# Adding up the squares of the first RMS norm: TensorE matmuls in one bank in place of GpSimd additions

## The chip, the cores and the metric

The kernel runs on one core of one Trainium2 chip, as one launch. The metric is the device time of a run in microseconds (us), lower is better. A core has TensorE for matmuls (PE in the profile, with its weight loads listed apart as PEld), VectorE (DVE), ScalarE (ACT), GpSimd (POOL) and SyncE (SP), which here only issues transfers. Each engine works through its own queue in order; a wait at the head of a queue holds everything behind it.

## The reference

Two layers of a decoder trunk over 512 tokens of 1024 features, everything in float32:

```python
def hybrid_layer(h, p_i, ...):
    xn = rms_norm(h, g_mix)
    proj = xn @ w_in                    # c_q, keys, values, gates, mLSTM inputs
    c_q = rms_norm(c_q, g_cq)           # then queries and index queries from c_q
    att = dsa_attention(...)            # top-k keys for each query, softmax, values
    hm = sigmoid(m_o) * rms_norm(mlstm_chunkwise(...), g_mh)
    h = h + concat([att, hm]) @ w_out
    h = h + square(relu(rms_norm(h, g_mlp) @ w_ff1)) @ w_ff2
    return h + sigmoid(rms_norm(h, g_ple) @ w_ple_gate + b) * (p_i @ w_ple)

def rms_norm(x, g):
    return x * rsqrt(mean(x * x, axis=-1) + 1e-6) * g
```

The change touches the first `rms_norm` of the first layer alone: the sum over 1024 features of the squares of each token.

## The kernel before

The state `h` lies feature-major: 8 blocks of 128 features (partitions) by 512 tokens. Float32 products are made of three single-precision passes: every operand is split into a rounded part `hi` (ACT) and a rest `lo` (DVE), and `mm3` or `token_step` issue hi·hi, hi·lo and lo·hi into one PSUM bank.

The norm is not applied before the projections. `prep` multiplies block k by the gain and splits it; the factor r of each token (the reciprocal root) is multiplied in when a projection is copied out of PSUM. So the matmuls need no r, but the copies after them do. `prep` also squares each block on ACT (L589) and adds the squares on GpSimd, seven additions in a chain (L594). `token_r` (L599) then multiplies the one sum with a column of ones: four float32 matmuls of a 128 x 128 block by one column, each giving the sums of 128 tokens in one column of a bank. From this bank DVE works out r in about a dozen tiny steps (`rsqrt`, L550), and `spread` (L613) makes a row of it.

Work is grouped in stages: mix, mlp and ple of layer 0 are stages 0, 1 and 2, those of layer 1 are 3, 4 and 5. The mix stage first projects `cq` (2 feature blocks: 8 x 2 x 3 = 48 matmuls of 512 columns) and `keys` (4 token blocks: 8 x 4 x 3 = 96 matmuls of 336 columns); then come the index queries, the top-k choice on DVE, queries, values, the convolution, attention, the mLSTM and the output projection. The squares of `cq` have a norm of their own, with four more one-column matmuls.

The program's order is made by a planner (`Plan.schedule`, L250). It goes through the work in simulated time with a cost for each operation and gives each free engine the ready operation of highest rank; the rank is the path to the end plus a thousand times the number that `URGENT` (L51) gives the operation's label. Labels that matter here are `start` 325 (splits of the first blocks and weights), `norm` 180, `squares0` 90, `cq` 80, `keys` 55, `queries` 45, `index` 30 and `values` 30. The order found is then written out as fixed, so on the chip each engine waits in that order whatever is ready. A buffer lives from its first writer to its last reader: weights come through three `raw` buffers, freed when DVE has made the `lo` part, into four `hi` and four `lo` buffers, freed when the last matmul has read them. Of the 8 PSUM banks, the 4 of keys and the 2 of cq are in use early on. All instructions are written out at one line (L395), so the profile tells them apart by tiles: `s` are 128 x 512 buffers, `raw`, `hi`, `lo` weights, `const` what stays (h, gains, ones), `ps_tr` a bank for norms and transposes.

Of the kernel before, what the change touches and what calls it, by code (L numbers as in the profile page):

```python
# [27 lines left out]
NTB = S // 128  # L28
# [378 lines left out]
class Trunk:  # L407
# [159 lines left out]
    def prep(self, l, gcol, forms=None):  # L567


        nc = self.nc  # L570
        label = nc.label
        cf = self.cf[l][0]
        xs, acc, last = [], None, None
        for k in range(KD):
            nc.label, nc.bias = ("prep", 0) if nc.stage else ("start", -STEP * k)
            hi, lo = self.slot([128, S], F32R), self.slot([128, S], F32R)
            self.split_block(self.h[k], cf[:, gcol + k:gcol + k + 1], hi, lo)
            if forms is not None:
                nc.label = "forms"
                x = self.slot([128, S])  # L580
                nc.scalar.activation(x, self.h[k], AF.Copy, scale=cf[:, gcol + k:gcol + k + 1])
                if k % 2:
                    forms.append(self.right_sums(last, x))
                last = x
            nc.bias = 0
            xs.append((hi, lo))
            nc.label = "squares" if nc.stage else "squares0"
            sq = self.slot([128, S])
            nc.scalar.activation(sq, self.h[k], AF.Square)  # L589
            if acc is None:  # L590
                acc = sq
            else:
                nacc = self.slot([128, S])
                nc.gpsimd.tensor_tensor(nacc, acc, sq, op=ALU.add)  # L594
                acc = nacc
        nc.label = label
        return xs, acc

    def token_r(self, acc, dim):  # L599

        nc = self.nc
        label, nc.label = nc.label, "norm"
        ps = self.psum("tr")
        for tb in range(NTB):
            nc.tensor.matmul(ps[:, tb:tb + 1], acc[:, tb * 128:(tb + 1) * 128], self.ones[:, 0:1],
                             start=True, stop=True)
        v = self.tiny([128, NTB])
        nc.vector.tensor_scalar(v, ps[:, 0:NTB], 1.0 / dim, EPS, op0=ALU.mult, op1=ALU.add)
        r = self.rsqrt(v, [128, NTB])
        nc.label = label  # L610
        return r
# [818 lines left out]
```

## Time and profile before

| | |
|---|---|
| median of 3 runs | 1330.98 us (1330.89 to 1331.20) |
| the profiled execution: its own time | 1332.49 us |
| the profiled execution: span from first to last instruction | 1330.5 us |
| mean granted TensorE clock | 0.996 |
| TensorE busy | 1305.7 us (98%) |
| VectorE busy | 1016.6 us (76%) |
| ScalarE busy | 725.2 us (55%) |
| GpSimd busy | 141.5 us (11%) |

The profiled execution took 1.5 us longer than the median of the runs; 2.0 us of it lie outside the span. The busy time of PE counts a matmul from its start to its modelled end, so two that overlap look busy without a gap; the distance from one weight load to the next is the better price of a matmul. The granted clock is 1.00 where TensorE has its higher level (2.4 GHz) and 0.50 at its lower (1.2 GHz).

### The profile page before, as it was taken

Reading aid. Unit: us, or ns where it says so; the run is one execution under the profiler, and the core shown is the slowest. Engines: PE = TensorE matmul, PEld = TensorE weight load, DVE = VectorE, ACT = ScalarE, POOL = GpSimd, SP = SyncE. Lnnn points to the kernel's source line nnn. Section 1 sums busy time; section 2 is a strip of 40 time slices with the busy share of each in tenths; the row PEclk is TensorE's granted clock in tenths of the full one; section 3 lists DMA queues with packets and bytes.
Section 4 is the critical chain, followed back from the end, with each engine's and each line's share of the span. In section 5 each row is a group of like instructions: output and inputs, shape, how many; then the busy total and the mean of one; then the engine's idle time right before and its main releaser. Section 6 shows DMA issues by size and latency. Waiting matters only on the chain. (4 is left out here: it accounts for less than half of the span.)

```text
span 1330.5 us, 19866 instructions
## 1 busy us (share of the span) xinstructions
PE 1305.7 (98%) x7376; PEld 1124.3 (85%) x7376; DVE 1016.6 (76%) x2122; ACT 725.2 (55%) x1403; POOL 141.5 (11%) x161
## 2 busy tenths in 40 slices
PE   6999999999999999999999999999999999999998
PEld 5877889888989899988887777988898898899887
DVE  7799997697777767763858999968877777767635
ACT  4887586474444434355448955847644444434542
POOL 4132000120000000004113211003000000000210
PEclk9999999999999999999999999999999999999999
DMA  5547610353323332335234674113433323333441
GB/s 195 119 112 181 159 49 2 95 127 111 97 95 111 96 111 82 109 127 130 82 100 114 140 176 112 48 33 99 124 107 99 111 90 101 96 111 95 127 121 70
DMA packets 41569, 141.76 MB, mean 107 GB/s; under 512 B 4992, under 2 KB 5504, under 8 KB 41472
## 3 DMA queue, kind: packets, MB, share of 16 engines
q1 hardware_dynamic: 34848, 116.37, 27.7%
q0 software_dynamic: 6624, 24.12, 9.9%
q8 instruction: 58, 0.95, 0.3%
q14 instruction: 39, 0.32, 0.1%
HBM read 114.25 MB, written 2.10 MB: 87 GB/s over the span
## 5 line engine op out<-in xcount | busy, mean ns | idle before, releaser
L395 PE MATMUL ps_proj<-s,hi 128*128 128x512 f32 (+1 forms) x3184 | 845.0, 355 | 2.7 <-DVE s L395 2.3
L395 PEld LDWEIGHTS ps_proj<-s,hi 128*128 128x128 f32 x3184 | 557.5, 189 | 90.7 <-DVE s L395 2.7
L395 PE MATMUL ps_proj<-s,lo 128*128 128x512 f32 (+1 forms) x1592 | 560.5, 355 | 0.5 <-DVE lo L395 0.5
L395 ACT ACTIVATE hi<-raw 128x1024 fp32r<-128x1024 f32 (+1 forms) x212 | 222.4, 1052 | 309.3 <-PE ps_proj L395 264.8
L395 PEld LDWEIGHTS ps_proj<-s,lo 128*128 128x128 f32 x1592 | 300.0, 189 | 45.6 <-DVE lo L395 1.3
L395 DVE TENSOR_TENSOR lo<-raw,hi 128x1024 fp32r<-128x1024 f32 (+1 forms) x165 | 202.9, 1230 | 83.9 <-ACT hi L395 76.3
L395 DVE TENSOR_TENSOR const<-const,ps_proj 128x512 f32<-128x512 f32 x160 | 109.6, 686 | 90.7 <-PE ps_proj L395 90.5
L395 PE MATMUL ps_proj<-hi,s 128*128 128x512 f32 (+1 forms) x384 | 112.8, 380 | 8.3 <-ACT hi L395 7.5
L395 POOL TENSOR_TENSOR s<-s,s 128x512 f32<-128x512 f32 x42 | 63.1, 1502 | 506.7 <-ACT s L395 494.5
L395 PEld LDWEIGHTS ps_proj<-hi,s 128*128 128x128 f32 x384 | 69.9, 193 | 18.7 <-ACT hi L395 7.5
L395 ACT ACTIVATE s<-s 128x512 fp32r<-128x512 f32 (+2 forms) x138 | 78.2, 620 | 13.8 <-DVE s L395 9.2
L395 PE MATMUL ps_sc<-s,s 128*128 128x512 f32 (+3 forms) x288 | 84.3, 375 | 0.6 <-ACT s_idx L395 0.2
L395 DVE TENSOR_TENSOR s<-s,s 128x512 fp32r<-128x512 f32 (+2 forms) x108 | 68.1, 667 | 9.0 <-ACT s L395 9.0
L395 POOL DMA_DIRECT2D lo<-raw x46 | 40.2, 873 | 295.8 <-ACT lo L395 237.3
L395 PE MATMUL ps_proj<-lo,s 128*128 128x512 f32 (+1 forms) x192 | 65.9, 382 | 1.8 <-DVE lo L395 1.7
L395 ACT ACTIVATE s<-const,const 128x512 fp32r<-128x512 f32 x64 | 44.2, 713 | 35.0 <-DVE const L395 35.0
L395 DVE SCALAR_TENSOR_TENSOR s<-const,const,s 128x512 fp32r<-128x512 f32 x48 | 48.0, 1009 | 17.0 <-ACT s L395 17.0
L395 ACT ACTIVATE s<-ps_proj 128x256 f32<-128x256 f32 (+1 forms) x104 | 42.8, 420 | 32.9 <-PE ps_proj L395 32.5
L395 PEld LDWEIGHTS ps_sc<-s,s 128*128 128x128 f32 x288 | 50.5, 190 | 8.8 <-ACT s_idx L395 1.5
L395 ACT ACTIVATE hi<-at 128x1024 fp32r<-128x1024 f32 x28 | 29.7, 1061 | 51.4 <-PE ps_proj L395 47.5
L395 DVE TENSOR_TENSOR s<-s,ps_proj 128x256 f32<-128x256 f32 x84 | 35.2, 419 | 26.7 <-PE ps_proj L395 23.3
L395 ACT ACTIVATE lo<-raw 128x1024 fp32r<-128x1024 f32 x46 | 48.8, 1062 | 9.7 <-PE ps_proj L395 6.0
(150 smaller groups left out, 1603.6 us busy)
## 6 DMA issues: line engine op xcount, KB each, us to landing
raw<-ws SPq DMA_DIRECT2D x204, 512.0 KB, 3.5
lo<-raw POOLq DMA_DIRECT2D x46, 512.0 KB, 5.1
raw<-wa SPq DMA_DIRECT2D x8, 336.0 KB, 3.6
const<-xt SPq DMA_DIRECT2D x8, 256.0 KB, 4.6
s<-pt SPq DMA_DIRECT2D x8, 256.0 KB, 4.6
out<-const SPq DMA_DIRECT2D x7, 256.0 KB, 2.0
const<-ct SPq DMA_DIRECT2D x2, 132.0 KB, 3.2
out<-const SPq DMA_DIRECT2D x2, 128.0 KB, 1.7
```

Of the source, the lines that this page charges most:

```text
L395: ins = getattr(getattr(nc, e), method)(*[value(x) for x in args], **{k: value(x) for k, x in kw.items()}).ins
```

## The change

In stage 0 the squares are no longer added by GpSimd. `prep` hands the list of the eight squares on, and `token_r` issues four one-column matmuls for each of them, all 32 into the same four columns of one bank, which TensorE adds up in PSUM. The first matmul of the first block alone opens the bank (`start`), those of the last block close it. In all other stages the sum is made as before, and `cq`, `keys` and the rest are not touched.

```diff
@@ prep
             sq = self.slot([128, S])
             nc.scalar.activation(sq, self.h[k], AF.Square)
-            if acc is None:
+            if not nc.stage:
+
+                acc = (acc or []) + [sq]
+            elif acc is None:
                 acc = sq
             else:
                 nacc = self.slot([128, S])
@@ token_r
         ps = self.psum("tr")
-        for tb in range(NTB):
-            nc.tensor.matmul(ps[:, tb:tb + 1], acc[:, tb * 128:(tb + 1) * 128], self.ones[:, 0:1],
-                             start=True, stop=True)
+        parts = acc if isinstance(acc, list) else [acc]
+        for k, part in enumerate(parts):
+            for tb in range(NTB):
+                nc.tensor.matmul(ps[:, tb:tb + 1], part[:, tb * 128:(tb + 1) * 128], self.ones[:, 0:1],
+                                 start=k == 0 and (tb == 0 or len(parts) == 1), stop=k == len(parts) - 1,
+                                 skip_group_check=len(parts) > 1)
```

The planner takes every operation anew, so the written order can change wherever its simulated times do.

## Rows read from the trace of the kernel before

**Rows 1.** The page's part 1: busy time, share of the span, instructions of each engine.
```profile
PE 1305.7 (98%) x7376; PEld 1124.3 (85%) x7376; DVE 1016.6 (76%) x2122; ACT 725.2 (55%) x1403; POOL 141.5 (11%) x161
```

**Rows 2.** Stretches of the first mix stage: busy us of each engine, granted clock, DMA.
```profile
core 0: us, PE busy (x) PEld busy (x) DVE busy (x) ACT busy (x) POOL busy (x), PEclk, DMA share, GB/s
25.00:29.00 4.00, 4.00 (x11) 3.14 (x12) 4.00 (x36) 0.00 (x0) 0.00 (x0) 0.57 0.75 243
30.40:37.10 6.70, 6.70 (x32) 5.57 (x31) 0.00 (x0) 1.62 (x3) 0.00 (x0) 1.00 0.00 0
54.00:60.00 6.00, 4.67 (x28) 3.81 (x29) 4.96 (x27) 6.00 (x23) 0.00 (x0) 1.00 0.67 158
60.00:80.00 20.00, 19.86 (x118) 16.43 (x117) 18.12 (x55) 18.16 (x65) 7.56 (x5) 1.00 0.36 80
80.00:100.00 20.00, 17.24 (x90) 13.42 (x89) 19.81 (x54) 17.01 (x44) 5.41 (x7) 1.00 0.50 122
100.00:104.00 4.00, 4.00 (x12) 3.11 (x11) 4.00 (x15) 3.77 (x9) 1.03 (x3) 0.57 1.04 240
```

**Rows 3.** Who waited for whom from 0 to 40 us: total us, times, longest.
```profile
PEld ps_proj L395 <- DVE lo L395: 3.7, 4, 1.6
```

**Rows 4.** Groups by shape: DVE and POOL to 20.1 us, then DVE from 20.1 to 24.95.
```profile
L395 DVE SCALAR_TENSOR_TENSOR s<-const,const,s 128x512 fp32r<-128x512 f32 x7 | 10.1, 1479 | 1.3 <-ACT s L395 1.3
L395 DVE TENSOR_TENSOR lo<-raw,hi 128x672 fp32r<-128x672 f32 x4 | 5.1, 1276 | 0.4 <-ACT hi L395 0.4
...
L395 POOL TENSOR_TENSOR s<-s,s 128x512 f32<-128x512 f32 x7 | 11.0, 1578 | 4.1 <-ACT s L395 3.9
...
L395 DVE TENSOR_TENSOR lo<-raw,hi 128x672 fp32r<-128x672 f32 x1 | 0.8, 846 | 0.0
```

**Rows 5.** Timeline of ACT, DVE and SP's transfers: start us, us, operation.
```profile
4.42 0.61 ACT L395 ACTIVATE s<-const 128x512 f32<-128x512 f32 x1
...
6.16 0.61 ACT L395 ACTIVATE s<-const 128x512 f32<-128x512 f32 x1
...
14.44 0.71 ACT L395 ACTIVATE s<-const,const 128x512 fp32r<-128x512 f32 x1
...
15.05 1.14 ACT L395 ACTIVATE s<-const 128x512 f32<-128x512 f32 x2
...
18.37 2.79 SPq L395 DMA_DIRECT2D raw<-ws  x2
...
20.73 0.74 DVE L395 SCALAR_TENSOR_TENSOR s<-const,const,s 128x512 fp32r<-128x512 f32 x1
...
21.95 1.06 ACT L395 ACTIVATE hi<-raw 128x1024 fp32r<-128x1024 f32 x1 [4.19 <-DMA raw<-ws]
...
23.73 1.22 DVE L395 TENSOR_TENSOR lo<-raw,hi 128x1024 fp32r<-128x1024 f32 x1
...
36.07 1.06 ACT L395 ACTIVATE hi<-raw 128x1024 fp32r<-128x1024 f32 x1 [3.99 <-PE ps_proj L395]
```

**Rows 6.** Timeline of TensorE's weight loads, one for each pass: start us, us, count.
```profile
7.48 1.06 PEld L395 LDWEIGHTS ps_proj<-hi,s 128*128 128x128 f32 x4 [7.48 <-ACT hi L395]
...
15.54 1.27 PEld L395 LDWEIGHTS ps_proj<-hi,s 128*128 128x128 f32 x8
...
21.57 1.01 PEld L395 LDWEIGHTS ps_tr<-const,s 128*128 128x128 f32 x8
...
33.58 0.87 PEld L395 LDWEIGHTS ps_proj<-s,hi 128*128 128x128 f32 x4
...
42.69 0.19 PEld L395 LDWEIGHTS ps_up<-hi,s 128*128 128x128 f32 x1
```

**Rows 7.** The norm of layer 1: its one-column passes (PEld), then the stretch behind them.
```profile
678.13 0.97 PEld L395 LDWEIGHTS ps_tr<-const,s 128*128 128x128 f32 x8 [1.37 <-POOL s L395]
...
680.00:684.00 4.00, 4.00 (x12) 3.10 (x12) 2.78 (x13) 0.00 (x0) 0.00 (x0) 0.57 0.00 0
```

## The prediction
> **What bounds the kernel now.** I read the page's busy shares first, then the first mix stage in stretches, then who waited for whom, the groups by shape, and the timeline engine by engine. TensorE is busy for 1305.7 of 1330.5 us [rows 1], so a microsecond of matmuls put into a full stretch costs a microsecond, and the question is how much idle or slow TensorE time lies where the change works. There is some in the first 43 us. The 144 matmuls of keys and cq, which the first index matmul at 42.69 us stands behind, begin at 7.48 us [rows 6]: 35.2 us. Their content I price by the distance of weight loads, (length of a run - 0.19) / (count - 1), where 0.19 us is one load. A 336-column matmul takes (1.27 - 0.19) / 7 = 0.154 us, a 512-column one (0.87 - 0.19) / 3 = 0.227, and a one-column float32 matmul makes two passes of (1.01 - 0.19) / 7 = 0.117, so the four of one block take 0.94 us [rows 6], in layer 1 0.89 [rows 7]; I take 0.92. Keys are 96 x 0.154 = 14.8, cq 48 x 0.227 = 10.9, the norm of the squares 0.92, that of cq 0.92, the two 512-column matmuls of `spread` 0.45: 28.0 us. So 7.2 of the 35.2 us are lost. Waits for a rest (`lo`) from VectorE take 3.7 [rows 3]; from 25 to 29 us the granted clock is 0.57, which costs 4 x 0.43 = 1.7 [rows 2]; the other 1.8 is the slow beginning, whose first four key matmuls stand (1.06 - 0.19) / 3 = 0.29 apart instead of 0.154 [rows 6], and small waits.
>
> VectorE is late because of GpSimd. While the seven additions run (11.0 us, mean 1578 ns), the rest of a block takes 1479 ns on VectorE, and that of a keys weight 1276 [rows 4]; with GpSimd idle they take 737 (0.74) [rows 5] and 846 ns [rows 4]. VectorE's row of rests ends at 20.73 + 0.74 = 21.47 us, though ScalarE had the last block's `hi` done at 14.44 + 0.71 = 15.15 [rows 5]. The lateness goes on through the buffers: the transfer of cq's second weight is issued only at 18.37, when a rest has freed its `raw` buffer; ScalarE waits 4.19 us for it and has its `hi` at 23.0, VectorE its `lo` at 24.95 [rows 5]. From 30.4 to 37.1 us VectorE then has nothing at all to do [rows 2]: ScalarE's next copy is held until cq's last matmul frees a weight buffer at 36.07 [rows 5].
>
> **What is removed.** Seven GpSimd additions, 11.0 us of an engine that is busy for 11% of the span: worth nothing by themselves. Their shadow on VectorE is worth more. At the idle prices the last rests end at 15.15 + 0.85 + 0.74 = 16.7 us at the latest, instead of 21.47. ScalarE's row is unchanged, since the same 8 squares and 12 `hi` parts stay in it. The third keys rest, which frees the buffer for cq's second weight, then comes 4 to 5 us earlier, and with it that weight: its `lo` is ready at about 20 instead of 24.95. One more thing goes: all squares are done at 15.05 + 1.14 = 16.2 us [rows 5], and the norm no longer waits for a chain of additions behind them.
>
> **What is added.** 28 one-column matmuls, 56 passes: 7 blocks x 0.92 = 6.4 us of TensorE. Where do they lie? The label `norm` (180) ranks over cq (80) and keys (55), so each block of four goes into TensorE's order soon after its square. Block 0's square is ready at 4.42 + 0.61 = 5.03 us, block 1's at 6.77 [rows 5], when TensorE has not begun: its first key matmul waits for ScalarE until 7.48 [rows 6]. These two blocks are mostly hidden by that wait. What a one-column pass takes at the beginning's slow rate no row shows: between 0.92 us for a block, as at full speed, and twice that, 1.84, as with the 336-column matmuls (0.29 against 0.154). So block 1 ends between 6.77 + 0.92 = 7.7 and 5.03 + 2 x 1.84 = 8.7 us. The other six stand among key matmuls and are on the path. The rest of the work is then 6 x 0.92 = 5.5, keys 14.8, cq 10.9, cq's norm 0.92, `spread` 0.45: 32.6 us, ending between 40.3 and 41.3 if TensorE neither waits nor slows.
>
> The waits for VectorE I take at nothing, because with 6.4 us more to do TensorE is now behind VectorE (rests done by 16.7, cq's by 20, while keys alone would fill it to 23): if that cover failed they would cost up to the 3.7 of now. The slow beginning costs between 0 (TensorE starts 2.4 us sooner, and may be at speed sooner) and the 1.8 of now; I take 0.9. The dip at 25 to 29 us, behind TensorE's waits, I take as gone, since no wait is left ahead of it. That gives 41.2 to 42.2, middle 41.7; 0.3 more for the new waits of TensorE for a square at the head of its queue (behind such a wait stand key matmuls that could have run; a square takes 0.61 and ScalarE runs ahead of TensorE) makes 42.0 instead of 42.69 us: a gain of 0.7. The bank that the norm opens is now held from the first block to the last, beside keys' four and cq's two; an eighth is left for `spread`, so it costs nothing. The squares live longer in buffers; the additions' outputs, one for each, go.
>
> **What is moved.** cq outranks keys, and its weights come 5 us earlier, so its 10.9 us now run from about 20 to 31 and the keys end last. The buffer that ScalarE waited for until 36.07 then comes 5 us earlier, and VectorE and ScalarE can do the rests and copies behind cq in their idle 6.7 us [rows 2]. After 42.69 TensorE still has idle time: 1.3 us from 54 to 60, 0.1 to 80, 2.8 to 100, and a clock of 0.57 from 100 to 104 costs 1.7 [rows 2]: 5.9 us, while VectorE is at 18.1 and 19.8 of 20 us [rows 2]. How much of it closes no row shows. Between all of it (-5.9) and as much again lost by a new written order (+3, half the sum); I take a gain of 0.7, nearer to nothing because the copies of keys, which lead to the top-k chain, cannot come earlier than the keys matmuls. Beyond 104 us TensorE is nearly gapless and shifts as a whole.
>
> The sum: -0.7 - 0.7 = -1.4 us. On the profiled execution's 1332.49 us that is 1331.1; against the median of the runs, 1330.98, from which that execution stood off by 1.5 us, it is 1329.6.
>
> **The clock speaks against the change.** From 5 to 17 us about half of TensorE's time would be one-column passes. Behind the only norm block of layer 1, which follows a wait of 1.37 us, the granted clock is 0.57 for 4 us [rows 7], though TensorE then ran without a gap; behind a block and waits it is 0.57 at 25 to 29 as well [rows 2]. The Trainium skill, "TensorE: Matmul & The Clock Gate", section Part 1: The HAM clock gate, says that the default state is throttled and that activity releases it. It does not say that a one-column matmul counts like a wide one; by that rule, if it does not, the start stays slow. This is the first rival.
>
> **The rivals.**
> Slower: the clock stays at 1.2 GHz (half) through the interleaved stretch, until cq's wide matmuls come. The price: some 30 key matmuls x (0.29 - 0.154) = 4.1 us, and the six blocks 0 to 5.5 more; against the forecast's 0.9 for a slow beginning and without its later gain, -0.7 - 0.9 + 4.1 = +2.5 at least, taken as +3.5: 1334.5. It decides if the half rate lasts beyond about 15 us. Against it: the key matmuls came to speed within 8 us of their start although they waited for VectorE.
> Faster: the later idle closes. With VectorE and ScalarE ahead by 5 us at 37, 3.5 of the 5.9 us go: -0.7 - 3.5 = -4.2, 1326.8; with all of it and no slow beginning 1323.5.
> It does not do what it says: if the blocks are not spread but stand together behind the last square, the two first are not hidden; then TensorE starts at 7.48 with 34.4 us of work and 1.8 lost: 43.7, +1.0, and the median is 1332.0. What speaks for it is that cq's norm matmuls stand together now; against it, their inputs come together.
>
> **How the numbers follow.** A measurement of this kernel can tell about 0.2% (2.7 us) from no change: faster is below 1328.3, slower above 1333.6. The forecast (1328.4 to 1332 with its bounds) has 0.36, the faster rival 0.32, blocks together 0.08, the slow clock 0.16, and 0.08 goes to a written order that loses more than it gains (+3 on top of the forecast's start: 1333.9). That makes faster 0.32, same 0.44, slower 0.24. The forecast is 1329.6. The range leaves out the lower end of the faster rival and the upper end of the slow clock, about 1 in 10 each: 1325 to 1335.5.
>
> **What the profile afterwards would show.** Right, if VectorE's rests of blocks fall from 1479 to about 740 ns, its row ends before 17 us, cq's second `lo` is ready near 20, one-column loads count 64 in the first 20 us, beginning near 5.0, GpSimd has 154 instructions and TensorE 7432, and the first `ps_up` load comes near 42. Wrong, if the granted clock or the distance of key matmuls shows half speed after 12 us (then the first rival), if `ps_up` is near 42 but the idle after 54 us differs much from 4.2 us (then the moved order decides), or if TensorE waits for squares by more than 1 us.

## The result, and the profile after

The changed kernel takes 1339.56 us (median of 4 runs, 1339.02 to 1339.99) against 1330.93 for the kernel before (four runs as well): 8.6 us more, a ratio of 1.0062 with a 95% interval of 1.0050 to 1.0073. The forecast was 1329.6. The span of its profiled execution is 1337.5 us, 7.0 more than before.

The page's part 1 of the changed kernel, as [rows 1]:

```profile
PE 1316.1 (98%) x7432; PEld 1138.8 (85%) x7432; DVE 1010.6 (76%) x2125; ACT 725.7 (54%) x1400; POOL 131.2 (10%) x154
```

TensorE has the 56 passes more that the change says, and 10.4 us more busy time. GpSimd has lost its seven additions, and VectorE is relieved, as this group by shape (5 to 20.1 us, of after; to be read beside [rows 4]) shows:

```profile
L395 DVE SCALAR_TENSOR_TENSOR s<-const,const,s 128x512 fp32r<-128x512 f32 x8 | 5.9, 748 | 2.6 <-ACT s L395 2.6
L395 DVE TENSOR_TENSOR lo<-raw,hi 128x672 fp32r<-128x672 f32 x4 | 3.4, 859 | 1.5 <-ACT hi L395 1.5
```

The rest of a block takes 748 ns and not 1479, that of a keys weight 859 and not 1276. VectorE's last rest of a block, in its timeline:

```profile
15.48 0.75 DVE L395 SCALAR_TENSOR_TENSOR s<-const,const,s 128x512 fp32r<-128x512 f32 x1
```

ends at 16.2 us instead of 21.5. What went wrong stands on TensorE. This is the timeline of its weight loads in the changed kernel (start us, us, count), with the first index matmul at the end, as in [rows 6]:

```profile
5.74 3.49 PEld L395 LDWEIGHTS ps_tr<-const,s 128*128 128x128 f32 x16 [5.74 <-issue]
9.11 0.33 PEld L395 LDWEIGHTS ps_proj<-hi,s 128*128 128x128 f32 x1
9.36 1.85 PEld L395 LDWEIGHTS ps_tr<-const,s 128*128 128x128 f32 x8
...
12.71 1.89 PEld L395 LDWEIGHTS ps_tr<-const,s 128*128 128x128 f32 x8
...
22.03 3.60 PEld L395 LDWEIGHTS ps_tr<-const,s 128*128 128x128 f32 x16
25.51 0.33 PEld L395 LDWEIGHTS ps_proj<-lo,s 128*128 128x128 f32 x1
25.72 2.29 PEld L395 LDWEIGHTS ps_proj<-hi,s 128*128 128x128 f32 x8
27.97 1.17 PEld L395 LDWEIGHTS ps_proj<-lo,s 128*128 128x128 f32 x4
...
31.32 0.19 PEld L395 LDWEIGHTS ps_proj<-lo,s 128*128 128x128 f32 x1
...
51.33 0.19 PEld L395 LDWEIGHTS ps_up<-hi,s 128*128 128x128 f32 x1
```

Three things are to be seen. From 5.74 us on TensorE waits for nothing. One weight load takes 0.33 us until about 30 us and 0.19 later. And everything is slow alike until then: the passes of a block stand (1.89 - 0.33) / 7 = 0.223 us apart instead of 0.117, the key matmuls (2.29 - 0.33) / 7 = 0.28 instead of 0.154. That is the lower clock, 1.2 GHz, for some 24 us. The profile's granted clock does not say so here: it reads 1.00 throughout, as it also does over the slow first key matmuls of before; it seems to hold no reading before the first change that it records. The length of a load is the better witness, and `e3_in_a_row` below shows both together.

The sum closes on this to 0.4 us. 64 passes x (0.223 - 0.117) = 6.8 us, and the 38 key matmuls issued up to 29.9 us x (0.28 - 0.154) = 4.8: 11.6 us lost. The work at full speed was 34.4 us. 34.4 + 11.6 = 46.0, and from 5.74 to 51.33 us are 45.6. The first index matmul comes 8.6 us later than before.

Further on, some of this is made up. These are the `ps_pn` matmuls before and after (first and last start, us):

```profile
L395 PE MATMUL ps_pn<-vx,s_d x160: 272/275/349, 169.6 to 867.4; 128*128 128x129 f32 x160
L395 PE MATMUL ps_pn<-vx,s_d x160: 272/275/329, 177.5 to 874.4; 128*128 128x129 f32 x160
```

The first is 7.9 us later than before and the last 7.0, as the spans are. So it is in part by accident that 8.6 us is also the difference of the medians: the profiled execution of before was 1.5 us above its median. The idle time that the forecast hoped to close is not what made it up. The stretch from 54 to 104 us of before, and the same length 8 us later after the change (columns as in [rows 2]):

```profile
54.00:104.00 50.00, 45.77 (x242) 36.77 (x243) 46.89 (x148) 44.95 (x137) 13.99 (x14) 0.97 0.51 119
62.00:112.00 50.00, 45.81 (x243) 37.10 (x242) 48.55 (x148) 45.15 (x133) 13.29 (x13) 0.97 0.46 102
```

TensorE is idle for 4.2 us in both, and the mean granted clock is 0.97 in both: the idle time and the dip that stood at 100 us are still there, 8 us later (the granted clock is 0.60 from 108 to 112 us). Behind the norm of layer 1, where [rows 7] show 0.57 for 4 us, it is 1.00 in this execution (688 to 692 us), which may account for the last 0.9 us.

### The profile page after: what moved, and what is told of

It reads as the page before. It is cut to its first block, busy times and chain, and to the rows that moved or that the text cites. A ratio compares the mean times of both kernels' runs of the same rounds, so it can differ in the third digit from the quotient of the medians.

```text
span 1337.5 us, 19963 instructions
## 1 busy us (share of the span) xinstructions
PE 1316.1 (98%) x7432; PEld 1138.8 (85%) x7432; DVE 1010.6 (76%) x2125; ACT 725.7 (54%) x1400; POOL 131.2 (10%) x154
## 5 line engine op out<-in xcount | busy, mean ns | idle before, releaser
L395 PE MATMUL ps_proj<-hi,s 128*128 128x512 f32 (+1 forms) x384 | 116.2, 389 | 3.3 <-ACT s L395 3.3
L395 POOL TENSOR_TENSOR s<-s,s 128x512 f32<-128x512 f32 x35 | 52.5, 1500 | 502.8 <-ACT s L395 491.2
L395 DVE SCALAR_TENSOR_TENSOR s<-const,const,s 128x512 fp32r<-128x512 f32 x48 | 42.0, 881 | 18.1 <-ACT s L395 18.1
```

The source lines that it names most:

```text
L395: ins = getattr(getattr(nc, e), method)(*[value(x) for x in args], **{k: value(x) for k, x in kw.items()}).ins
```

## The experiments

My theory after reading this profile, the clock theory: one-column passes do not bring TensorE to its higher clock, and the blocks among the first key matmuls keep it at the lower one. Rivals: the work theory (a one-column float32 pass takes its 0.22 us by itself), the order theory (the planner's new order and GpSimd's missing part are the loss), and that taking the sum to TensorE is bad in itself.

**e1_neither** takes the additions away and adds nothing. In stage 0 the norm is made from the last block's squares:

```diff
-            nc.scalar.activation(sq, self.h[k], AF.Square)
-            if acc is None:
+            nc.scalar.activation(sq, self.h[k], AF.Square, scale=1.0 if nc.stage else 8 ** 0.5)
+            if acc is None or not nc.stage:
```

> Neither the GpSimd additions nor the added matmuls: the norm is taken from the last block's squares alone, scaled by 8, so seven blocks are left out of the sum. Clock theory (the change loses because one-column passes keep TensorE at its lower clock): without such passes key matmuls are 0.154 us apart by about 12 us, the first ps_up load comes at 38 to 39 us instead of 42.7 (before) and 51.3 (after), and the time is 1326 to 1328. Order theory (the change loses by the new written order and the loss of GpSimd's part as such): the first ps_up load near 43, the time 1331 or more. Work theory (the passes cost their 0.21 us each whatever the clock) gives the same as the clock theory here.

Measured: 1324.67 us against 1331.13, ratio 0.9948 (0.9933 to 0.9963). Two of its first weight loads, then those of the index matmuls (min/median/max ns, first and last start in us):

```profile
6.33 1.06 PEld L395 LDWEIGHTS ps_proj<-hi,s 128*128 128x128 f32 x4 [6.33 <-ACT hi L395]
...
12.00 1.26 PEld L395 LDWEIGHTS ps_proj<-hi,s 128*128 128x128 f32 x8
```

```profile
L395 PEld LDWEIGHTS ps_up<-hi,s x28: 187/188/190, 36.5 to 47.4; 128*128 128x128 f32 x28
```

The first index matmul stands at 36.5 us, 6.2 earlier than before: better than I expected. So what the change removes is worth 6.5 us, and doing without GpSimd's additions, with the new order that this brings, loses nothing. That speaks against the order theory; the changed kernel's own order is put to the test in e6_columns.

**e2_both** keeps GpSimd's additions beside the changed kernel's 32 matmuls.

```diff
                 acc = (acc or []) + [sq]
+                if last is not None:
+                    nacc = self.slot([128, S])
+                    nc.gpsimd.tensor_tensor(nacc, last, sq, op=ALU.add)
+                    sq = nacc
+                last = sq
```

> The 32 matmuls of the change, and GpSimd's seven additions kept beside them (their sum is not used). Clock theory: as after, passes about 0.21 us apart and half rate until about 28 us; VectorE's rests are slow again (1.3 to 1.5 us) but TensorE is slower still and does not wait for them; first ps_up load 51 to 53, time 1339 to 1341. If taking GpSimd's additions away were the cause, the time would be 1331 to 1334.

Measured: 1340.49 us, ratio 1.0066 (1.0049 to 1.0082). VectorE's groups by shape (5 to 21 us) show it slow again:

```profile
L395 DVE SCALAR_TENSOR_TENSOR s<-const,const,s 128x512 fp32r<-128x512 f32 x8 | 8.8, 1125 | 2.3 <-ACT s L395 2.3
L395 DVE TENSOR_TENSOR lo<-raw,hi 128x672 fp32r<-128x672 f32 x4 | 7.2, 1802 | 0.4 <-ACT hi L395 0.4
```

The index matmuls' loads:

```profile
L395 PEld LDWEIGHTS ps_up<-hi,s x28: 186/187/190, 50.8 to 65.0; 128*128 128x128 f32 x28
```

but the first index matmul stands at 50.8, no later than in the changed kernel. The matmuls alone make the loss; and VectorE's relief, worth 6.5 us in e1_neither, is worth at most 1 us behind a TensorE that is later still.

**e3_in_a_row** turns the order of the blocks, so that the first of the 32 matmuls needs the last square and none can stand among the early key matmuls.

```diff
-        parts = acc if isinstance(acc, list) else [acc]
+        parts = acc[::-1] if isinstance(acc, list) else [acc]
```

> The same 32 matmuls, but the block of the last square first, so that all stand in one row behind the last square (16 us) and none among the early key matmuls. Clock theory: the keys in front come to 0.154 us by about 12 us as in before, the 64 passes take 0.117 us each (7.5 us), the clock falls behind them for some 4 us (1.7 lost); first ps_up load 43.5 to 46, time 1331.5 to 1335. Work theory (the passes cost 0.21 us each wherever they stand): 64 passes take over 13 us, first ps_up load near 51, time 1338 to 1341. Order theory: near 1339 too if keys and cq are pushed back as much.

Measured: 1337.35 us, ratio 1.0040 (1.0025 to 1.0055): a miss for all three. The five runs are spread, two at 1334.2 and 1335.0, three from 1337.4 to 1338.6; the profile is of the run of 1337.35. The weight loads show what happened, and here the granted clock has been recorded (the second fence is of stretches, with the columns of [rows 2]):

```profile
14.40 1.26 PEld L395 LDWEIGHTS ps_proj<-hi,s 128*128 128x128 f32 x8
...
15.93 1.01 PEld L395 LDWEIGHTS ps_tr<-const,s 128*128 128x128 f32 x8
...
17.12 10.22 PEld L395 LDWEIGHTS ps_tr<-const,s 128*128 128x128 f32 x56
```

```profile
17.50:20.00 2.50, 2.50 (x21) 2.50 (x21) 2.28 (x18) 0.00 (x0) 0.00 (x0) 0.84 0.85 261
20.00:30.00 10.00, 10.00 (x42) 9.42 (x42) 3.92 (x35) 1.06 (x1) 1.15 (x2) 0.50 0.38 92
```

The keys in front come to 0.154 us as before, and the first block's passes take 0.117 us, on the same squares and the same bank: the work theory is out. But in the row the granted clock falls to 0.50 while TensorE is busy without a gap, and stays there through the wide matmuls of cq that follow, until about 33 us. I had the clock fall behind the row; it fell inside it, so the 56 passes took 10.2 us, and the fall cost more than 1.7.

**e4_wide** lets TensorE add the squares with wide matmuls: one of 512 columns with the identity for each block, a copy of the bank, and then the four one-column matmuls of before. The squares are rounded for the single pass (the line for this is left out here).

```diff
...
+        if isinstance(acc, list):
+            total = self.psum("tr")
+            for k, part in enumerate(acc):
+                nc.tensor.matmul(total, self.identr, part, start=k == 0, stop=k == len(acc) - 1)
+            acc = self.slot([128, S])
+            nc.scalar.activation(acc, total, AF.Copy)
         ps = self.psum("tr")
-        parts = acc if isinstance(acc, list) else [acc]
+        parts = [acc]
```

> The sum still on TensorE and not on GpSimd, but by one 512-column single-precision matmul with the identity for each block (8 in all, into one bank), a ScalarE copy of the bank, and the old four one-column matmuls. The squares are rounded to single-pass precision. Clock theory: TensorE begins at about 5.7 us with wide matmuls, is at speed by 10 us and stays there; eight matmuls cost 0.23 to 0.45 us each; first ps_up load 39 to 41, time 1327 to 1329.5. If taking the sum to TensorE is the loss in itself (work on the full engine, or the new order), the time is above 1333.

Measured: 1327.09 us, ratio 0.9971 (0.9961 to 0.9982): faster than both kernels. Its weight loads in order of time, then those of the index matmuls:

```profile
5.89 0.29 PEld L395 LDWEIGHTS ps_tr<-s,const 128*128 128x128 f32 x1 [5.89 <-ACT s L395]
...
9.92 1.28 PEld L395 LDWEIGHTS ps_proj<-hi,s 128*128 128x128 f32 x8
11.21 0.19 PEld L395 LDWEIGHTS ps_tr<-s,const 128*128 128x128 f32 x1
```

```profile
L395 PEld LDWEIGHTS ps_up<-hi,s x28: 186/188/190, 37.4 to 50.8; 128*128 128x128 f32 x28
```

TensorE begins at 5.89, loads take 0.19 from 10 us on, and the first index matmul stands at 37.4. The sum on TensorE is not bad in itself.

**e6_columns** is the decisive one. It is the changed kernel with 128 columns of ones in place of one: the same weights, float32 passes and places, and more work. (A line that picks one column of each result is left out here.)

```diff
-                nc.tensor.matmul(ps[:, tb:tb + 1], part[:, tb * 128:(tb + 1) * 128], self.ones[:, 0:1],
+                n = 128 if len(parts) > 1 else 1
+                nc.tensor.matmul(ps[:, tb * n:(tb + 1) * n], part[:, tb * 128:(tb + 1) * 128], self.ones[:, 0:n],
...
```

> The change with 128 moving columns of ones in place of one in each of the 32 added matmuls, all else alike (same weight loads, same float32 passes; one column of each result is used). More work, not less. Clock theory, that the moved columns are what one-column passes lack: TensorE is at its higher clock by about 10 us in spite of it, passes 0.12 to 0.25 us apart, key matmuls 0.154 us by 12 us, first ps_up load 42 to 46, time 1330 to 1335. If float32 passes do not raise the clock whatever their columns: key matmuls stay 0.28 us apart past 20 us, time 1339 to 1343.

Measured: 1330.94 us against 1331.08, ratio 0.9998 (0.9987 to 1.0010). Its weight loads in order of time, then those of the index matmuls:

```profile
6.02 3.48 PEld L395 LDWEIGHTS ps_tr<-const,s 128*128 128x128 f32 x16 [6.02 <-issue]
...
9.94 1.20 PEld L395 LDWEIGHTS ps_tr<-const,s 128*128 128x128 f32 x8 [0.22 <-ACT s L395]
...
11.78 1.01 PEld L395 LDWEIGHTS ps_tr<-const,s 128*128 128x128 f32 x8
...
18.84 1.25 PEld L395 LDWEIGHTS ps_proj<-hi,s 128*128 128x128 f32 x8
```

```profile
L395 PEld LDWEIGHTS ps_up<-hi,s x28: 186/188/189, 42.4 to 56.7; 128*128 128x128 f32 x28
```

The first 16 passes are as slow as in the changed kernel (3.48 us against 3.49), but from 10 us on a block takes 1.01 us and key matmuls 0.154. With 127 columns more in every added matmul the kernel is 8.6 us faster, and no execution crosses over: ten runs took 1327.8 to 1331.9, the four of the changed kernel 1339.0 to 1340.0. Its written order is that of the changed kernel but for a few places, so the order theory falls too. Moved columns are all that was added, and with them TensorE comes to its higher clock 20 us earlier; what the changed kernel lost against before is gone (ratio 0.9998).

**e5_warmed** and **e8_warmed_longer** set 14 and 32 plain matmuls of 128 columns ahead of everything (the diff is that of the first; the second has 32 in the loop), to have the clock up when the first block comes.

```diff
+        ps, label, nc.label, nc.bias = self.psum("tr"), nc.label, "start", 400
+        for _ in range(14):
+            nc.tensor.matmul(ps[:, 0:128], self.onesr, self.onesr, start=True, stop=True)
+        nc.label, nc.bias = label, 0
```

> The change, with 14 matmuls of 128 x 128 by 128 columns issued ahead of all other TensorE work, so that TensorE is at its higher clock when the first one-column block comes; their result is not used. Clock theory in its strong form (one-column passes also let a high clock fall): passes are 0.117 us apart at first, then 0.21 to 0.23 again, key matmuls 0.28 until past 20 us, time 1335 to 1339. In its weak form (only the start is slow, a clock once up stays up among one-column passes): passes 0.117 us, first ps_up load near 42, time 1330 to 1332.5. If the passes cost 0.21 us by themselves: 1339 to 1341.

> As e5_warmed with 32 matmuls of 128 columns ahead in place of 14: in e5_warmed the 14 ended at 5.5 us with the clock still low, so it did not show what a high clock does among one-column blocks. The 32 last until about 8 us and bring the clock up. If a high clock falls among interleaved one-column blocks (clock theory, strong form): loads of 0.33 us again before 20 us, 1336 to 1341 in most runs. If it stays up there and only the rise is at stake (weak form): passes 0.117 us apart throughout, first ps_up load 43 to 45, all runs 1331 to 1334, in one group.

Measured: e5_warmed 1340.81 us, in two groups: 8 of 10 runs took 1340.1 to 1342.0, two 1331.2 and 1332.2. e8_warmed_longer 1344.96, all four within 0.6. The weight loads of e5_warmed (the profile is of the run of 1331.2) and then of e8_warmed_longer:

```profile
2.46 3.06 PEld L395 LDWEIGHTS ps_tr<-const 128*128 128x128 f32 x14 [2.46 <-ACT const L395]
5.75 3.49 PEld L395 LDWEIGHTS ps_tr<-const,s 128*128 128x128 f32 x16 [0.24 <-issue]
...
11.86 1.10 PEld L395 LDWEIGHTS ps_tr<-const,s 128*128 128x128 f32 x8
...
18.90 1.90 PEld L395 LDWEIGHTS ps_tr<-const,s 128*128 128x128 f32 x16
```

```profile
2.46 4.98 PEld L395 LDWEIGHTS ps_tr<-const 128*128 128x128 f32 x23 [2.46 <-ACT const L395]
7.31 1.83 PEld L395 LDWEIGHTS ps_tr<-const,s 128*128 128x128 f32 x8
```

Neither did what it was for: the plain matmuls did not bring the clock up, 23 of them in 5 us did not, so no high clock met the first blocks. Once the clock rose, in the profiled execution of e5_warmed at about 12 us, it stayed up among the blocks, one-column passes and all. So the same program can end in either group; what decides between them I have not found. Of the eight longer runs there is no trace, so that it is the clock there too is inferred from their times. The median falls in the range that I had set for the work theory, which e3_in_a_row has ruled out; the two shorter runs are in that of the weak form. Both forecasts for e8_warmed_longer missed. Whether a high clock would always live through the interleaved blocks stays open.

**e7_wide_both** uses e4_wide's matmuls in the mix stage of layer 1 as well (`nc.stage % 3` in place of `nc.stage` in the two tests).

> As e4_wide, with the 512-column identity matmuls in the first mix stage of both layers. Clock theory: in layer 1 the norm's wait for GpSimd and the stretch of lower clock behind it (about 1.4 and 1.7 us) go, against 8 x 0.23 = 1.8 us more of TensorE in a full stretch: 1325.5 to 1327.5, at most 1.5 better than e4_wide. If it is idle at the start that makes e4_wide pay, layer 1 loses the 1.8: 1328 to 1329.5.

Measured: 1327.40 us, ratio 0.9979 (0.9969 to 0.9989), the same as e4_wide within the interval. At the norm of layer 1 the wait for GpSimd (1.31 us in e4_wide) and the lower clock behind it (granted 0.71 from 676 to 680 us) are gone, against 8 x 0.23 = 1.8 us of matmuls: they cost about what they save.

Put together, in medians: the additions' removal gives 1331.1 - 1324.7 = 6.5 us; the added matmuls as work take back 1330.9 - 1324.7 = 6.3 (e6_columns less e1_neither, which both have a short slow beginning); the longer time at the lower clock costs 1339.6 - 1330.9 = 8.6 on top.

## Why the prediction was wrong

- *VectorE's relief*: right. Rests at 748 and 859 ns, the row's end at 16.2 us (at the latest 16.7 was said), no wait of TensorE for VectorE up to the first index matmul.
- *The added work at full speed*: right in size. 6.4 us were worked out, 6.3 are between e6_columns and e1_neither. That they agree so well is in part luck: both runs begin at the lower clock, and what this costs them nearly cancels. By my estimate from their weight loads, e6_columns takes 5.0 us up to 11.05 us for work that is 3.0 at full speed and 0.2 of waiting, e1_neither 5.1 us up to 11.38 us for work that is 2.9. With the clock up, e6_columns has its first index matmul at 42.4 us, where 42.0 was forecast, and 1330.9 us.
- *The slow beginning*: this step failed. It was taken as 0.9 us, between 0 and 1.8, on the ground that TensorE starts sooner and may be at speed sooner. It starts sooner, at 5.74 us, and is at the lower clock until about 30 us; some 11 us are lost. Both ends of that bound came from before, where wide matmuls alone stood in the beginning. They could not bound a beginning that is half one-column passes, and [rows 7] and the dip in [rows 2] were there to say so.
- *The first rival*: right in its mechanism, wrong in its price and its chance. The sign that I had named for it, key matmuls at half speed after 12 us, is there. It had 4.1 us for key matmuls and "0 to 5.5" for the six blocks; measured are 4.8 and, for all eight blocks, 6.8. With its own upper end the rival comes to -0.7 - 0.9 + 4.1 + 5.5 = +8.0 us, 1339.0. I took +3.5, near the lower end, with the point that at the lower clock a pass might still take 0.117 us; no row said that it might, and the slow key matmuls in the rows nearly doubled (0.29 against 0.154). The slow stretch also puts off what I had expected to end it: cq's wide matmuls, which I had at about 20 us, began at 29.9. The range should have reached this end.
- *The two first blocks hidden by the wait to 7.48 us*: half right. They began at 5.74, since the planner put ScalarE's first `hi` ahead of the first square, and ended at 9.1 (8.7 was the upper bound).
- *cq from 20 to 31 us*: wrong, without effect on TensorE, which never waited. cq's weight buffers were freed by key matmuls, and these were late; this row is of ScalarE in the changed kernel:

```profile
27.36 1.06 ACT L395 ACTIVATE hi<-raw 128x1024 fp32r<-128x1024 f32 x1 [11.04 <-PE ps_proj L395]
```

- *The later idle time*: the forecast had 0.7 of 5.9 us closing. None closed: the 4.2 us of idle time and the dip came 8 us later as they were.
- *The dip at 25 to 29 us* was taken as gone. There is no separate dip in the changed kernel: TensorE had been at the lower clock since its start and stayed there until about 30 us.
- *A slip in the rivals' sums*: a gain of 0.7 and a loss of 3 by the written order come to +2.3, 1333.3 us and not 1333.9. That lies below the 1333.6 from which I counted as slower, so its 0.08 belonged to "same".

The Trainium skill, "TensorE: Matmul & The Clock Gate", Part 1: The HAM clock gate, says that the default state is throttled and that activity releases the throttle. The runs agree with its first half: in the changed kernel weight loads take 0.33 us in the beginning. With its second half they agree only in part: TensorE was busy without a gap from 5.74 us on and stayed at its lower clock until about 30 us; in e6_columns, with columns to move, it left it by 10.

## What to carry to other kernels

The stream of matmuls with one moving column was priced twice here: its passes, and the clock of everything around it. Before small matmuls are used to fill an idle start, ask whether the engine is at speed there and what would bring it to speed; if a sum must go to TensorE, give it wide matmuls (an identity matmul of 512 columns for each block: 1327.1 us here, against 1330.9 and 1339.6). And when a rival's price has two ends, take the end to which all neighbouring rows point, and let the range reach it.

## What the runs showed of the hardware

- 127 more moved columns in each of 32 float32 matmuls made the program 8.6 us faster (1330.94 against 1339.56).
- The granted clock fell from 1.00 to 0.50 in the middle of a gapless row of one-column passes (e3_in_a_row, at about 19.5 us), and stayed there through the first 5 us of wide matmuls behind it.
- 23 matmuls of 128 columns in 5 us did not bring the clock up (e8_warmed_longer), while in e1_neither it came up by 12 us after key matmuls of 336 columns from 6.3 us on.
- A weight load takes 0.33 us where the granted clock is 0.50 and 0.19 where it is 1.00 (e3_in_a_row); in the first 30 us of the changed kernel loads take 0.33 under a recorded 1.00.
- Beside GpSimd's additions VectorE's rest of a block (128 x 512) took 1479 ns instead of 748, and that of a keys weight 1276 instead of 859.
